# A decoder trunk's last feed-forward: down projection kept feature-major, the residual turned inside the last matmul groups

## Chip, cores and metric

The kernel runs on one core of a Trainium2 chip. The metric is the device time of one execution in microseconds. The kernel before has a median of 1202.2 us over three runs, from 1201.6 to 1202.57.

## The reference

Two layers over 512 tokens of width 1024, everything in float32. Layer 0 mixes tokens with forgetting attention, layer 1 with differential attention, and each adds cross-attention into 256 memory tokens. Every layer ends like this, and this is where the change lies:

```python
x = x + mix @ w_out[layer]
x = x + swiglu(rmsnorm(x, ffn_norm_g[layer]), w_gate_up[layer], w_down[layer])
...
return rmsnorm(x, final_norm_g)
```

Here `swiglu` is `(silu(h @ w_gate) * (h @ w_up)) @ w_down`, with 2816 hidden columns. The result of the last `rmsnorm` is stored with tokens as rows.

## The kernel before, in words

Activations lie feature-major: 128 features on the partitions, 512 tokens along the row, eight such blocks for width 1024. Each float32 operand is split into a high and a low part in the matmul type `fp32r`, and a product of two operands is three matmuls: high by high, low by high, high by low. The high part is a cast on ACT, the low part a subtraction on DVE, so every weight piece passes ACT, then DVE, before its low part can be used.

**Output projection** (`out_proj`, lines 588 to 614). Four quarters `o` of 256 output features, in PSUM tiles with the tags `acc`, `sc`, `y` and `tr`, one after the other. Each quarter is 48 matmuls of 512 columns (lines 199 to 201), over four weight chunks in the order 6, 0, 2, 4. For chunks 0 and 4 (`by_dma`), ACT writes the negated high part (L180), and a POOL DMA adds the raw weights onto it (L182); for the others, ACT casts (L165) and DVE subtracts (L166). After a quarter, DVE adds the residual (L603, L604), ACT multiplies by the norm's gain (L608), and `make` (L560 to L570) builds the operands of the feed-forward: `xh`, `xl`, and the sums `sh`, `sl`. Before the fourth quarter, `ahead()` loads the first three gate-and-up weight tiles (`FirstThree`); two of them get a second load added onto the first by POOL (L797).

**Residual.** In layer 0 it stays feature-major in `qs.block`, and its squares are summed on ACT and DVE (`squares`, L237 and L238). In layer 1 each block of the new residual is put into a scratch tile, turned to rows by four PE transposes (L619, into PSUM, 32 in all), copied to `res` by ACT (L620), and squared by row (L625); `norm_of_rows` brings the norm back to columns with a fp32 matmul (L637).

**Feed-forward** (`ffn`). Eleven quads of 256 hidden columns, gate and up together. Each quad is seven products of 24 matmuls of 256 columns (lines 835 to 837). The first three of the first quad (`first products` below: `acc`, `y` and `sc`, 72 matmuls) are put in program order after the output projection, and the tile scheduler lets some of them go ahead of it. Each quad's `p` copy (L881) follows its first product. Down projection pieces are filled in between the products of later quads (`fill`): in layer 0 feature-major, 12 matmuls of 512 columns (lines 943 to 945) per piece and an add on DVE; in layer 1 token-major, 24 matmuls of 256 columns (lines 934 to 936) and an add on DVE (L939). Pieces of the first group are half as long. In layer 1 the last four hidden blocks' share is computed by `final` (L975): for each of four token tiles and two halves, 12 matmuls of 512 columns (lines 991 to 993), DVE adds the residual row (L996), ACT squares (L998), DVE multiplies by the gain (L1005), then scales and stores.

**What sets the order.** The tile scheduler lays out each engine's queue, in order, from the program's order and its estimate of when things are ready; `with behind(pe)` keeps what stands in it behind the PE instruction issued last. Each engine then runs its queue strictly in order, and a waiting instruction holds all behind it.

## Time and profile before

| | before |
|---|---|
| median of three runs | 1202.2 us |
| profiled execution | 1206.7 us |
| its span | 1204.9 us |
| PE busy | 1168.8 us, 97% |
| DVE busy | 993.7 us, 82% |
| ACT busy | 662.8 us, 55% |
| POOL busy | 159.1 us, 13% |

PE is TensorE's matmuls, PEld its weight loads, DVE VectorE, ACT ScalarE, POOL GpSimd. The span runs from the first to the last instruction of the profiled execution; the execution's own time is 1.8 us longer. Times inside the trace count from the span's start. A matmul's length in the timeline overlaps the next one; the distance between starts is what it costs.

### The profile page before, as it was taken

Reading aid. Unit: us, or ns where it says so; the run is one execution under the profiler, and the core shown is the slowest. Engines: PE = TensorE matmul, PEld = TensorE weight load, DVE = VectorE, ACT = ScalarE, POOL = GpSimd, SP = SyncE. Lnnn points to the kernel's source line nnn. Section 1 sums busy time; section 2 is a strip of 40 time slices with the busy share of each in tenths; the row PEclk is TensorE's granted clock in tenths of the full one; section 3 lists DMA queues with packets and bytes.
Section 4 is the critical chain, followed back from the end, with each engine's and each line's share of the span. In section 5 each row is a group of like instructions: output and inputs, shape, how many; then the busy total and the mean of one; then the engine's idle time right before and its main releaser. Section 6 shows DMA issues by size and latency. Waiting matters only on the chain.

```text
span 1204.9 us, 21021 instructions
## 1 busy us (share of the span) xinstructions
PE 1168.8 (97%) x7854; PEld 1064.8 (88%) x7854; DVE 993.7 (82%) x1708; ACT 662.8 (55%) x1207; POOL 159.1 (13%) x154
## 2 busy tenths in 40 slices
PE   8999999999999999999999999997999999999997
PEld 7888888779999999999887888876899999999996
DVE  5879987789997787778789999977699878777776
ACT  7658776665443333333456979776554333333334
POOL 0002001121221111110001020112121111111000
PEclk9999999999999999999999999998999999999999
DMA  7533233466786666664133234455668666656512
GB/s 237 143 84 88 72 84 97 126 142 157 177 204 162 154 153 157 153 154 120 57 111 115 76 103 121 105 148 106 157 158 199 162 148 158 152 144 152 148 53 88
DMA packets 163065, 160.46 MB, mean 133 GB/s; under 512 B 12993, under 2 KB 152698, under 8 KB 162962
## 3 DMA queue, kind: packets, MB, share of 16 engines
q1 hardware_dynamic: 136722, 131.83, 36.7%
q0 software_dynamic: 26240, 27.27, 15.7%
q8 instruction: 62, 1.02, 0.4%
q14 instruction: 41, 0.34, 0.1%
HBM read 142.23 MB, written 2.10 MB: 120 GB/s over the span
## 4 chain that ended last, share of the span: by engine, by line
PE 74%; DVE 10%; ACT 5%; DMA 5%; issue 4%; SPq 1%; POOL 0%; ACTq 0%; DVEq 0%; POOLq 0%
PE acc L837 4%; PE acc L835 4%; PE acc L836 4%; PE y L837 4%; PE y L836 4%; PE y L835 4%; PE tr L943 3%; PE tr L944 3%; PE tr L945 3%; PE sc L836 3%; PE sc L837 3%; PE sc L835 3%; PE tr L936 3%; PE tr L934 3%; PE tr L935 3%
## 5 line engine op out<-in xcount | busy, mean ns | idle before, releaser
L228 ACT CAST fhi<-raw 128x1024 fp32r<-128x1024 f32 (+1 forms) x202 | 208.1, 1034 | 283.4 <-PE sc L837 100.9
L229 DVE TENSOR_TENSOR flo<-raw,fhi 128x1024 fp32r<-128x1024 f32 (+1 forms) x202 | 241.2, 1198 | 33.5 <-ACT fhi L228 33.4
L797 POOL DMA_DIRECT2D raw<-in_w_gate_up_dram x88 | 107.4, 1455 | 472.1 <-DMA raw<-in_w_gate_up_dram 288.5
L170 ACT ACTIVATE whi<-raw,gains 128x256 fp32r<-128x256 f32 (+1 forms) x192 | 86.6, 503 | 38.6 <-PE acc L201 22.0
L835 PE MATMUL acc<-xh,fhi 128*128 128x256 f32 x352 | 100.2, 285 | 5.6 <-ACT xh L228 5.6
L837 PE MATMUL acc<-xl,fhi 128*128 128x256 f32 x352 | 100.2, 285 | 0.6 <-DVE xl L229 0.5
L171 DVE SCALAR_TENSOR_TENSOR wlo<-raw,gains,whi 128x256 fp32r<-128x256 f32 (+1 forms) x192 | 87.2, 493 | 16.4 <-ACT whi L170 14.7
L836 PE MATMUL acc<-xh,flo 128*128 128x256 f32 x352 | 99.2, 282 | 0.0
L936 PE MATMUL tr<-flo,ah 128*128 128x256 f32 x288 | 81.3, 282 | 0.0
L934 PE MATMUL tr<-fhi,ah 128*128 128x256 f32 x288 | 81.1, 282 | 0.0
L935 PE MATMUL tr<-fhi,al 128*128 128x256 f32 x288 | 81.1, 282 | 0.0
L835 PE MATMUL y<-sh,fhi 128*128 128x256 f32 x256 | 72.7, 284 | 1.7 <-ACT sh L228 1.7
L835 PEld LDWEIGHTS acc<-xh,fhi 128*128 128x128 f32 x352 | 67.2, 191 | 7.0 <-ACT xh L228 6.5
L837 PE MATMUL y<-sl,fhi 128*128 128x256 f32 x256 | 72.8, 284 | 0.2 <-DVE sl L229 0.2
L836 PE MATMUL y<-sh,flo 128*128 128x256 f32 x256 | 72.6, 284 | 0.0
L943 PE MATMUL tr<-ah,fhi 128*128 128x512 f32 x176 | 69.2, 393 | 0.0
L944 PE MATMUL tr<-ah,flo 128*128 128x512 f32 x176 | 69.1, 393 | 0.0
L945 PE MATMUL tr<-al,fhi 128*128 128x512 f32 x176 | 68.8, 392 | 0.0
L837 PEld LDWEIGHTS acc<-xl,fhi 128*128 128x128 f32 x352 | 67.1, 191 | 1.6 <-DVE xl L229 1.4
L836 PEld LDWEIGHTS acc<-xh,flo 128*128 128x128 f32 x352 | 67.3, 191 | 0.4
L199 PE MATMUL acc<-xh,whi 128*128 128x512 f32 x168 | 66.7, 398 | 0.2 <-DVE qk L732 0.2
L200 PE MATMUL acc<-xh,wlo 128*128 128x512 f32 x168 | 66.3, 395 | 0.0
(482 smaller groups left out, 3787.6 us busy)
## 6 DMA issues: line engine op xcount, KB each, us to landing
raw<-in_w_gate_up_dram SPq DMA_DIRECT2D x220, 256.0 KB, 3.3
raw<-in_w_gate_up_dram POOLq DMA_DIRECT2D x88, 256.0 KB, 5.9
raw<-in_w_down_dram SPq DMA_DIRECT2D x80, 256.0 KB, 3.7
raw<-in_w_out_dram SPq DMA_DIRECT2D x32, 256.0 KB, 3.2
raw<-in_a_w_in_dram SPq DMA_DIRECT2D x48, 128.0 KB, 2.3
raw<-in_w_kv_shared_dram SPq DMA_DIRECT2D x24, 256.0 KB, 3.2
raw<-in_w_mem_kv_dram SPq DMA_DIRECT2D x16, 256.0 KB, 3.0
raw<-in_a_w_in_dram SPq DMA_DIRECT2D x16, 256.0 KB, 3.8
```

The costliest lines, as they stand in the source:

```text
L228: act.copy(h, src)
L229: dve.tensor_sub(l, src, f32(h))
L797: pool.dma_start(t[:, k : k + 2], plus[:, k : k + 2], accum_op=ALU.add)
L835: pe.matmul(o, hi[:, e, uc], ah, start=u == 0 and e == 0, stop=False)
L836: pe.matmul(o, lo[:, e, uc], ah, start=False, stop=False)
L837: pe.matmul(o, hi[:, e, uc], al, start=False, stop=u == 1 and e == NP - 1)
L934: pe.matmul(o, h[:, tc_], hi[:, k], start=t % 2 == 0 and k == 0, stop=False)
L935: pe.matmul(o, l_[:, tc_], hi[:, k], start=False, stop=False)
L936: pe.matmul(o, h[:, tc_], lo[:, k], start=False, stop=t % 2 == 1 and k == nk - 1)
L943: pe.matmul(b, hi[:, k, oc], h, start=k == 0, stop=False)
L944: pe.matmul(b, lo[:, k, oc], h, start=False, stop=False)
L945: pe.matmul(b, hi[:, k, oc], l_, start=False, stop=k == nk - 1)
```

## The change

In layer 1 the residual now stays feature-major, as in layer 0: squares are summed by `squares`, the norm is `finish_norm` for both layers, and `turn_rows`, `row_squares` and `norm_of_rows` are gone. The down projection is feature-major in both layers: 432 matmuls of 512 columns replace 864 of 256. In `final`, four plain fp32 matmuls of a residual block by the identity are added to each PSUM group, 32 in all, so that the residual is turned and added there; ACT squares and DVE multiplies straight from PSUM. And the first products of the first quad stand in a `with behind(pe)`, in both layers: they are queued behind the output projection's last matmul.

```diff
...
     def out_proj(l, yh, yl, order, qs, sc, ahead):
 
         acc = tmp("xacc")
-        late, xg = [], None
         for o in range(4):
             bs = two_banks(("acc", "sc", "y", "tr")[o])
             if o == 3:
                 ahead()
             project([(w_out[l], o * 256, 256)], None, yh, yl, bs, NKB, order=order, by_dma=(0, 4))
-            for f in late:
-                f()
-            late = []
+            xg = sc.full("g")
             for j in range(2):
                 kb = 2 * o + j
-                xn = qs.block(kb) if l == 0 else sc.next_half()
+                xn = qs.block(kb)
                 dve.tensor_add(xn, bs[j], f32(xh[:, kb]))
                 dve.tensor_add(xn, xn, f32(xl[:, kb]))
-                if j == 0:
-                    xg = sc.full("g")
                 g = gains[:, G_FFN[l] + kb : G_FFN[l] + kb + 1]
                 act.activation(xg[:, j], xn, AF.Copy, scale=g)
-                if l == 0:
-                    squares(xn, acc, kb == 0)
-                else:
-                    late.append(lambda kb=kb, xn=xn: turn_rows(kb, xn, qs.rows()))
+                squares(xn, acc, kb == 0)
             qs.make(o, xg, sc.full("u").rearrange("p a c -> p (a c)")[:, : 3 * H])
-        return acc, late
...
+        return acc
...
             bp1, bp7, bp6 = bank("acc"), bank("y"), bank("sc")
             if q == 0:
-                for es in (range(NP - 1), range(NP - 1, NP)):
-                    product(bp1, "a11", w.w11, es)
-                    product(bp7, "s3", w.wt3, es)
-                    product(bp6, "s2", w.wt2, es)
                 with behind(pe):
-                    if last:
-                        for f in late:
-                            f()
-                        row_squares(qs.rows(), ss, 1)
-                    else:
-                        finish_norm(acc, False, bank("tr"))
+                    for es in (range(NP - 1), range(NP - 1, NP)):
+                        product(bp1, "a11", w.w11, es)
+                        product(bp7, "s3", w.wt3, es)
+                        product(bp6, "s2", w.wt2, es)
+                with behind(pe):
+                    finish_norm(acc, False, bank("tr"))
             else:
...
                 b = bank("tr")
-                if last:
-                    for t in (2 * (i % 2), 2 * (i % 2) + 1):
-                        tc_, o = slice(t * P, (t + 1) * P), b[:, (t % 2) * H : (t % 2) * H + H]
-                        for k, (h, l_) in enumerate(a):
-                            pe.matmul(o, h[:, tc_], hi[:, k], start=t % 2 == 0 and k == 0, stop=False)
-                            pe.matmul(o, l_[:, tc_], hi[:, k], start=False, stop=False)
-                            pe.matmul(o, h[:, tc_], lo[:, k], start=False, stop=t % 2 == 1 and k == nk - 1)
-                    t0 = 2 * (i % 2)
-                    dst = qs.rows()[:, t0 : t0 + 2, c * 256 : c * 256 + 256]
-                    dve.tensor_add(dst, halves(b), dst)
-                    return
                 oc = slice((i % 2) * P, (i % 2) * P + P)
                 for k, (h, l_) in enumerate(a):
                     pe.matmul(b, hi[:, k, oc], h, start=k == 0, stop=False)
...
-        final(w, blocks_of(GROUPS[-1]), qs.rows(), ring, sc)
-
-    def final(w, a, xtok, ring, sc):
+        final(w, blocks_of(GROUPS[-1]), qs, ring, sc)
+
+    def final(w, a, qs, ring, sc):
...
                     pe.matmul(o, h[:, c], hi, start=k == 0, stop=False)
                     pe.matmul(o, l_[:, c], hi, start=False, stop=False)
-                    pe.matmul(o, h[:, c], lo, start=False, stop=k == len(a) - 1)
+                    pe.matmul(o, h[:, c], lo, start=False, stop=False)
+                for i in range(4):
+                    x = qs.block(4 * e + i)[:, t * P : (t + 1) * P]
+                    pe.matmul(o[:, i * P : (i + 1) * P], x, ident, start=False, stop=i == 3)
                 for i, c in enumerate(cols):
                     if c.start // 512 == e:
-                        dve.tensor_add(xo[:, c], o[:, c.start - e * 512 : c.stop - e * 512], xtok[:, t, c])
+                        oc = o[:, c.start - e * 512 : c.stop - e * 512]
                         q = work()[:, :n]
-                        act.activation(q, xo[:, c], AF.Square, accum_out=s2[:, i : i + 1])
+                        act.activation(q, oc, AF.Square, accum_out=s2[:, i : i + 1])
+                        dve.tensor_mul(xo[:, c], oc, fg[:, c])
...
             act.activation(ry, ry, AF.Exp, scale=-0.5)
-            for c in cols:
-                dve.tensor_mul(xo[:, c], xo[:, c], fg[:, c])
             dve.tensor_mul(ra, ry, ry)
...
```

The change's new lines are L796 to L798 for the quad products, L593, L594 and L596 for what were L603, L604 and L608, L562 to L565 for L565 to L568, L780 for L819, and L931 to L936 for the last share.

PE's queue at the fourth quarter of layer 1's output projection. `tr` is its output, `whi` and `wlo` the parts of its weights, `sc` a first product. Before:

```order
L835 MATMUL sc_9800<-sh_9319,fhi_9665 128x256 [waits Activation_49]
L836 MATMUL sc_9800<-sh_9319,flo_9666 128x256 [waits DVE_49]
L837 MATMUL sc_9800<-sl_9320,fhi_9665 128x256
L835 MATMUL sc_9800<-sh_9319,fhi_9665 128x256
L836 MATMUL sc_9800<-sh_9319,flo_9666 128x256
L837 MATMUL sc_9800<-sl_9320,fhi_9665 128x256
L200 MATMUL tr_9641<-yh_b,wlo_9672 128x512 [waits DVE_49]
L201 MATMUL tr_9641<-yl_b,whi_9671 128x512
L200 MATMUL tr_9642<-yh_b,wlo_9672 128x512
```

After, from the end of the third quarter:

```order
L201 MATMUL y_9528<-yl_b,whi_9586 128x512
L199 MATMUL tr_9627<-yh_b,whi_9657 128x512 [waits Activation_49]
L199 MATMUL tr_9628<-yh_b,whi_9657 128x512
L200 MATMUL tr_9627<-yh_b,wlo_9658 128x512 [waits DVE_49]
L201 MATMUL tr_9627<-yl_b,whi_9657 128x512
L200 MATMUL tr_9628<-yh_b,wlo_9658 128x512
```

Before, 30 first products stand between the quarter's two L199 and its first L200 with the low part. Now that L200 is the third instruction after the third quarter, and the first products follow the quarter's 48th matmul. In layer 0 the move is smaller: eight first products go from ahead of the last ten output matmuls to behind them.

DVE's queue in the same place, around the subtraction L166 that makes this low part. Before:

```order
L566 TENSOR_TENSOR g_9624<-g_9624 128x256 [waits DVE_49]
L229 TENSOR_TENSOR flo_9666<-raw_9643,fhi_9665 128x1024 [waits Activation_49]
L567 TENSOR_TENSOR u_9630<-g_9624 128x256 [waits DVE_49]
L229 TENSOR_TENSOR xl<-g_9624,xh 128x512 [waits Activation_49]
L568 TENSOR_TENSOR u_9630<-g_9624,u_9630 128x256 [waits DVE_49]
L166 TENSOR_TENSOR wlo_9672<-raw_9669,whi_9671 128x512 [waits DMAHW5_49,DMASW7_49]
L166 TENSOR_TENSOR wlo_9709<-raw_9706,whi_9708 128x512 [waits DMAHW7_49,DMASW6_49,DMASW0_49]
L229 TENSOR_TENSOR sl_9320<-u_9630,sh_9319 128x768 [waits Activation_49]
```

After:

```order
L563 TENSOR_TENSOR g_9603<-g_9603 128x256 [waits DVE_49]
L229 TENSOR_TENSOR flo_9647<-raw_9632,fhi_9646 128x1024 [waits DMASW3_49,DMASW2_49]
L564 TENSOR_TENSOR u_9616<-g_9603 128x256 [waits DVE_49]
L229 TENSOR_TENSOR xl<-g_9603,xh 128x512 [waits Activation_49]
L565 TENSOR_TENSOR u_9616<-g_9603,u_9616 128x256 [waits DVE_49]
L780 TENSOR_TENSOR raw_9629<-raw_9629,raw_9632 128x1024
L229 TENSOR_TENSOR sl_9320<-u_9616,sh_9319 128x768 [waits Activation_49]
L166 TENSOR_TENSOR wlo_9658<-raw_9655,whi_9657 128x512 [waits DMAHW5_49,DMASW7_49]
L229 TENSOR_TENSOR flo_9652<-raw_9629,fhi_9651 128x1024 [waits Activation_49]
L166 TENSOR_TENSOR wlo_9695<-raw_9692,whi_9694 128x512 [waits DMAHW7_49,DMASW6_49,DMASW0_49]
```

Before, L166 stands ahead of the third quarter's `sl`; now it stands behind it, and 24 instructions lie between the `sl` of the first quarter and it: two `sl` of 768 columns, eleven of 512, eight of 256 and three of 1024. That first-quarter `sl` waits for ACT's `sh`, which ACT has behind the same cast of a POOL-loaded tile (`fhi`, L228) as before.

PE's queue in `final`, at the end of the first token tile's first half. Before:

```order
L991 MATMUL tr_13609<-fhi_13591,ah_13578 128x512
L992 MATMUL tr_13609<-fhi_13591,al_13579 128x512
L993 MATMUL tr_13609<-flo_13592,ah_13578 128x512
L991 MATMUL acc_13610<-fhi_13597,ah_13215 128x512 [waits Activation_49]
L992 MATMUL acc_13610<-fhi_13597,al_13216 128x512
```

After:

```order
L931 MATMUL tr_13116<-fhi_13098,ah_13085 128x512
L932 MATMUL tr_13116<-fhi_13098,al_13086 128x512
L933 MATMUL tr_13116<-flo_13099,ah_13085 128x512
L936 MATMUL tr_13116<-ident,res_9321 128x128 x4
L931 MATMUL acc_13117<-fhi_13104,ah_12770 128x512 [waits Activation_49]
```

Four matmuls of `res` by `ident` now end each group.

## Rows read from the trace of the kernel before

**Rows 1.** The page, busy us (share of the span) and instructions of each engine.
```profile
PE 1168.8 (97%) x7854; PEld 1064.8 (88%) x7854; DVE 993.7 (82%) x1708; ACT 662.8 (55%) x1207; POOL 159.1 (13%) x154
```

**Rows 2.** Busy time by stretch: from:to, length, then the engines', clock, DMA.
```profile
core 0: us, PE busy (x) PEld busy (x) DVE busy (x) ACT busy (x) POOL busy (x), PEclk, DMA share, GB/s
828.60:838.80 10.20, 7.54 (x27) 6.13 (x28) 10.14 (x19) 8.76 (x19) 0.89 (x1) 0.50 0.16 51
...
850.20:958.90 108.70, 105.96 (x884) 104.90 (x883) 97.76 (x118) 53.79 (x68) 21.72 (x18) 1.00 0.74 180
958.90:1147.30 188.40, 188.40 (x1586) 188.40 (x1585) 148.90 (x157) 71.71 (x73) 26.55 (x22) 1.00 0.61 149
273.40:379.00 105.60, 105.00 (x789) 99.99 (x788) 98.57 (x116) 50.18 (x56) 21.66 (x18) 1.00 0.74 179
379.00:564.60 185.60, 185.60 (x1299) 173.49 (x1298) 148.79 (x157) 71.80 (x73) 26.56 (x22) 1.00 0.62 152
```

**Rows 3.** Timeline of PE, layer 1: start, length, line, [idle before <-releaser].
```profile
822.40 0.40 PE L201 MATMUL y<-yl_b,whi 128*128 128x512 f32 x1
...
828.57 0.58 PE L835 MATMUL acc<-xh,fhi 128*128 128x256 f32 x1 [4.54 <-ACT xh L228]
...
832.75 0.58 PE L835 MATMUL y<-sh,fhi 128*128 128x256 f32 x1 [1.68 <-ACT sh L228]
...
839.19 0.50 PE L200 MATMUL tr<-yh_b,wlo 128*128 128x512 f32 x1
```

**Rows 4.** Chain of waits (start, us, what), then ACT's timeline, layer 1.
```profile
815.29 8.07 DMA raw<-in_w_gate_up_dram
...
823.44 1.05 ACT L228 CAST fhi<-raw 128x1024 fp32r<-128x1024 f32 x1 [4.50 <-DMA raw<-in_w_gate_up_dram]
...
825.43 0.83 ACT L228 CAST sh<-u 128x768 fp32r<-128x768 f32 x1
```

**Rows 5.** Timeline of DVE, layer 1, operands of the output projection's quarters.
```profile
825.64 1.22 DVE L229 TENSOR_TENSOR flo<-raw,fhi 128x1024 fp32r<-128x1024 f32 x1
826.78 0.95 DVE L229 TENSOR_TENSOR sl<-u,sh 128x768 fp32r<-128x768 f32 x1
827.65 0.68 DVE L603 TENSOR_TENSOR u<-y,xh 128x512 f32<-128x512 f32 x1
828.25 0.41 DVE L565 TENSOR_TENSOR u<-g 128x256 f32<-128x256 f32 x1
828.58 0.68 DVE L229 TENSOR_TENSOR xl<-g,xh 128x512 fp32r<-128x512 f32 x1
...
838.45 1.29 DVE L166 TENSOR_TENSOR wlo<-raw,whi 128x512 fp32r<-128x512 f32 x2
```

**Rows 6.** Timelines of PE and of ACT, layer 0, last quarter.
```profile
263.62 0.50 PE L200 MATMUL tr<-yh_a,wlo 128*128 128x512 f32 x1 [1.51 <-DMA wlo<-raw]
...
269.51 0.28 PE L835 MATMUL acc<-xh,fhi 128*128 128x256 f32 x1
...
270.81 0.51 PE L200 MATMUL tr<-yh_a,wlo 128*128 128x512 f32 x1 [0.21 <-DMA wlo<-raw]
...
265.72 0.63 ACT L180 ACTIVATE wlo<-raw 128x512 fp32r<-128x512 f32 x1
```

**Rows 7.** Timeline of PE, layer 1; last row: line L637's weight loads (ns, min/median/max).
```profile
814.99 1.07 PE L619 MATMUL tr<-ident,u 128*128 128x128 f32 x8
815.81 0.48 PE L201 MATMUL y<-yl_b,whi 128*128 128x512 f32 x1
...
874.15 1.16 PE L637 MATMUL tr<-work,ones 128*128 128x128 f32 x8 [2.07 <-DVE work L636]
875.07 0.36 PE L837 MATMUL acc<-xl,fhi 128*128 128x256 f32 x1
...
L637 PEld LDWEIGHTS tr<-work,ones x8: 187/192/193, 874.2 to 874.9; 128*128 128x128 f32 x8
```

**Rows 8.** Timeline of DVE and ACT at the end of the kernel.
```profile
1198.06 0.75 DVE L996 TENSOR_TENSOR u<-sc,res 128x256 f32<-128x256 f32 x2 [0.47 <-PE sc L993]
...
1198.52 0.42 ACT L998 ACTIVATE work<-u 128x256 f32<-128x256 f32 x1 [1.39 <-DVE u L996]
```

More of the change, by code (lines that the diff above doesn't have):

```diff
@@ L547, in block @@
             return self.x[:, kb * S : (kb + 1) * S]
-        def rows(self):
-            return self.x.rearrange("p (t d) -> p t d", t=NT)
         def operand(self, form, e):
@@ L575, in __init__ @@
         def __init__(self, pl):
-            self.pl, self.n = pl, 0
+            self.pl = pl
         def half(self, tag):
@@ L582, in full @@
             return self.pl.tile([P, 2, S], F32, tag=tag, name=nm(tag))
-        def next_half(self):
-            self.n += 1
-            return self.half(("p1", "u2", "u3")[self.n % 3])
     def out_proj(l, yh, yl, order, qs, sc, ahead):
         acc = tmp("xacc")
-        late, xg = [], None
         for o in range(4):
@@ L820, in __init__, with ffn @@
             self.wt2 = ring.parts(self.b11)
-    def ffn(l, acc, last, qs, late, ring, sc, pl, ahead):
+    def ffn(l, acc, last, qs, ring, sc, pl, ahead):
         raw, parts = ring.load, ring.parts
@@ L842, in ffn @@
         gated = {}
-        if last:
-            ss = tmp("ss", (P, 2, NT))
-            row_squares(qs.rows(), ss, 0)
         def quad(q, down):
@@ L888, in quad @@
             fill(1)
-            if q == 0 and last:
-                with behind(pe):
-                    norm_of_rows(ss)
             dve.tensor_add(b11, b11, b21)
@@ L1024, in output_and_ffn @@
             ahead = []
-            acc, late = out_proj(
+            acc = out_proj(
                 l, yh, yl, [6, 0, 2, 4], qs, sc, lambda: ahead.append(FirstThree(l, 0, ring))
@@ L1030, in output_and_ffn @@
             ring.far = open_pool(fs, f"f{l}", "right")
-            acc = ffn(l, acc, last, qs, late, ring, sc, open_pool(fs, f"a{l}"), ahead)
+            acc = ffn(l, acc, last, qs, ring, sc, open_pool(fs, f"a{l}"), ahead)
         if not last:
```

21 lines of the change are left out of this document (removed).

## Prediction

> **What bounds the kernel now.** I read the page's busy times first: PE (TensorE) works in 97% of the span, DVE in 82% [rows 1]. So a change counts where it adds or removes PE instructions, or makes PE wait. The busy time by stretch says where each is [rows 2]. Two stretches are fully packed in both layers: from the fifth quad's `p` copy to the eleventh's, PE is busy for 188.4 of 188.40 us in layer 1 and 185.6 of 185.60 us in layer 0. There only the number and kind of matmuls matter. The one place in layer 1 with a large hole is the passage from output projection to feed-forward: from 828.6 to 838.8 PE works 7.54 of 10.20 us, and at a granted clock of 0.50, which is the 1.2 GHz level; before and after it stands at 1.00.
>
> The timeline of PE shows why [rows 3]: the third quarter's last product starts at 822.40; then PE idles 4.54 us before 828.57 and 1.68 us before 832.75, and the fourth quarter's first low-part product (L200 with `wlo`) comes only at 839.19. The chain of waits names the start of it: a POOL accumulating load of `raw` takes 8.07 us from 815.29, ACT sits 4.50 us until its cast at 823.44, and the cast of `sh` is at 825.43 [rows 4]. DVE stands behind that cast, then works through third-quarter operands up to the two L166 subtractions at 838.45, the first of which makes that low part [rows 5]. So DVE's queue ends last there; its start-to-start times are 1.14 us for 1024 columns, 0.87 for 768, 0.60 for 512 and 0.33 for 256.
>
> **The change, part by part.**
>
> (a) End of the output projection, layer 1. Before, 30 first products ran while PE waited for the low part (they lie ahead of it in PE's order). Now nothing but two L199 products can. Worse, L166 has moved back in DVE's order: 24 instructions lie between the `sl` that waits for ACT's `sh` and L166: two more `sl`, eleven of 512 columns (among them square sums of layer 1, new on DVE), eight of 256, three of 1024. From 825.7 (the cast at 825.43 is now ahead by one `xh`, its end stays near) the sum with that first `sl` is 3×0.87 + 11×0.61 + 8×0.34 + 3×1.14 = 15.5 us; ACT's own queue (two gains, a square, a cast between each pair) adds about 0.8 us where the third quarter's gained block is awaited, and L166 itself takes 0.69. The low part is then there at 842.7, not 839.2: +3.5. PE will have been idle some 20 us, so I expect 1.2 GHz again when it resumes. The clock rose at 838.8, after 3.7 us of unbroken work from 835.1 [rows 2, 3]; the same after 842.7 costs 1.9 us of full-speed work. Bounds: nothing (the clock stays) and 5.1 us (the 10.2 us that the low level lasted in all). The next chunk's low part is accumulated by POOL; ACT issues its half at about 842.2, and in layer 0 PE got such a part 5.1 us after ACT's L180 started (265.72 to 270.81) [rows 6]: 847.3, when PE, at half speed, has done the ten products ahead of it by 846.9. +0.4. Together **+5.8** (3.5 to 9).
>
> (b) From there to the fifth quad's copy. The stretches of [rows 2] that begin at 850.2 and 273.4 begin where the last output product ends. Layer 1 now does what layer 0 does: 105.60 us there, 108.70 before, so −3.1. In this go 16 of the 32 transposes (L619, eight in 0.82 us), and the late wait of 2.07 us for DVE's L636 [rows 7]; the down matmuls become half as many of twice the width. But layer 0 had done eight first products (from 269.51 on, about 0.12 each [rows 6]) before its last ten output products; layer 1 now has done none: +0.95. Bounds −3.1 and −1.5; I take **−2.2**.
>
> (c) Fifth to eleventh quad: the same instructions as in layer 0: 185.6 − 188.4 = **−2.8**. Both are packed, so nothing hides this. By the loops this stretch holds 24 down pieces of 24 matmuls, and three more follow it: 3/24 of 2.8, **−0.35**.
>
> (d) The last share: 32 more matmuls, `x` block by identity, in plain fp32, on a PE that ends the kernel. The nearest row is L637, plain fp32, 128×128: four such matmuls (eight records) start at 874.15, and the next product at 875.07, 0.23 us each [rows 7]. 32 × 0.23 = **+7.4**. The lower bound is the price of a transposition of the same block, 0.10 us, 3.3 in all. For the upper bound, L637 loads the same `ones` for all its matmuls, and here each has its own block of `x` to load, in two loads; if those of 0.19 us [rows 7] were not covered by matmuls, a turn would take 0.38, 12.3 in all. I take L637, as it is the same kind of instruction and shape, and it too has two loads each. DVE's adds L996 fall away; they lay beside PE.
>
> The Trainium skill, Perfetto Trace Analysis, section Transposes, says that a logical transposition should use the transpose rather than a standard matmul. By this the change pays PE more than the 32 transposes it takes out (some 3.3 us); the two rows, 0.10 and 0.23, agree.
>
> (e) The tail. When PE's last product is done, DVE adds at 1198.06 and ACT squares at 1198.52 [rows 8]. Now ACT squares from PSUM when DVE would have begun: **−0.45**. The multiplication by the gain moves to DVE beside it.
>
> (f) Layer 0. Its eight first products filled the wait for the accumulated low part (270.81, idle 0.21 even so [rows 6]); now that wait is bare. At most 0.95; later waits in its first quads may take some back: **+0.6** (0 to 0.95).
>
> SP's and POOL's queues keep their order but for two down-weight loads, moved by one place: nothing, as these stretches are packed by PE.
>
> Sum: 5.8 − 2.2 − 2.8 − 0.35 + 7.4 − 0.45 + 0.6 = **+8.0 us**. The profiled execution took 1206.7, so 1214.7; the median of the runs, 1202.2, lies 4.5 below it, and the sum carried there gives **1210.2 us**.
>
> **The rivals.**
>
> *Faster: the low part is not late.* In layer 0 the same order ran the last quarter with a wait of 1.51 us before 263.62 and the one at 270.81, with the clock at 1.00. If layer 1 did that, the 48 products (0.23 each) would start by 822.6 and end near 835.4, where before they ended at 850.2: −14.8 in place of +5.8, and the total −12.6, **1189.6**. It decides at L166 ready by about 834.7, 8 us sooner than my chain. For it: the same code in layer 0. Against it: the load that holds ACT until 823.44 [rows 4] hangs on POOL's queue, whose order is unchanged, and DVE's 15.5 us come after it. 5%.
>
> *No change: the turn is cheap.* If a matmul by identity costs no more than a transposition, (d) is 3.3; with the clock term at nothing the sum is +2.0, **1204**. For it: L619 has the same operands. Against it: L637. 10%, 6% of it within 0.2%.
>
> *Dear: the weight loads of the turns are bare.* Then (d) is 12.3, the total +12.9, and the time **1215**. For it: new weights for each of the 32. Against it: L637 pays 0.23 with as many loads, and the matmuls ahead in the queue leave time to load. 7%. The Trainium skill, TensorE: Matmul & The Clock Gate, section Terms, gives transposition as 4× faster for fp32; by that figure and the 0.10 of L619, an estimate, a turn would take 0.41 and all 13.1, while the rows 0.23 and 0.10 are a ratio of 2.3.
>
> *The clock stays low longer.* At 10.2 us of half speed, 3.2 more: **1213.4**. It comes after a longer idle time than the one before. 15%.
>
> **How the numbers follow.** My forecast with its own bounds has 63%. 0.2% of the time, 2.4 us, is about what a measurement can tell from no change. Faster by more than that: the first rival and a little of small gains that I don't see, 0.06. Within: the cheap turn, or a low part that comes as before with all later gains, 0.09. Slower: the rest, 0.85. The range leaves out the faster rival and the dearest end: 1203.5 to 1216.
>
> **What would show it.** In the changed profile the first L200 of the fourth quarter in layer 1 should start at 842 to 843, not 839.19 [rows 3], the windows should show half clock after it for 3 to 5 us, the fifth to eleventh quad should take 185.6 us, the identity matmuls 0.23 us each, and the square of the last tile should start right after the last matmul. A low part before 838, or identity matmuls near 0.10 or 0.4, would make me wrong; so would packed stretches that don't come down to layer 0's.

## The result and the profile after

The changed kernel takes **1216.39 us** (median of four, 1215.8 to 1217.06), the kernel before 1202.38 beside it: a ratio of **1.0117**, with a 95% interval of 1.01 to 1.0135. That is 14.0 us slower; forecast were 8.0 us and 1210.2, with 1216.0 as the upper end. The sign and the mechanism named for it hold, the size does not.

The profiled execution of the changed kernel took 1215.8 us, so it is 9.1 us above the one that the prediction read (1206.7), near the 8.0. Most of the miss is thus not seen when these two traces are laid side by side, and the runs below search for it.

The page of the changed kernel, busy time, the line that answers to [rows 1]:

```profile
PE 1169.7 (96%) x7448; PEld 1048.2 (86%) x7448; DVE 994.1 (82%) x1700; ACT 659.4 (54%) x1190; POOL 159.1 (13%) x154
```

PE has 406 instructions fewer and works 0.9 us more. Busy time by stretch of the changed kernel, in the columns of [rows 2]: three pieces of layer 1's passage, then the stretches that answer to the last four rows there:

```profile
core 0: us, PE busy (x) PEld busy (x) DVE busy (x) ACT busy (x) POOL busy (x), PEclk, DMA share, GB/s
826.20:840.60 14.40, 0.00 (x0) 0.00 (x0) 14.40 (x25) 9.28 (x16) 0.00 (x0) 0.50 0.02 2
840.60:846.50 5.90, 5.87 (x14) 4.62 (x15) 1.71 (x2) 0.64 (x2) 1.77 (x2) 0.50 0.76 173
...
854.10:962.00 107.90, 106.94 (x797) 101.94 (x796) 99.04 (x116) 50.15 (x56) 21.72 (x18) 1.00 0.74 180
962.00:1148.90 186.90, 186.90 (x1298) 174.72 (x1298) 148.86 (x157) 71.86 (x73) 26.58 (x22) 1.00 0.62 150
269.60:377.80 108.20, 107.21 (x797) 102.00 (x796) 99.11 (x116) 50.33 (x57) 21.72 (x18) 1.00 0.73 175
377.80:564.60 186.80, 186.80 (x1298) 174.62 (x1297) 148.76 (x157) 71.80 (x72) 26.59 (x22) 1.00 0.62 150
```

In the passage PE does nothing for 14.4 us while DVE is busy in all of them, and then runs 5.9 us at the low clock. The last row is the one that nobody had named: layer 0's packed stretch, whose instructions the change leaves alone, went from 185.6 [rows 2] to 186.8, with the same count of matmuls to one.

The passage in the timelines of PE, ACT and DVE of the changed kernel (they answer to [rows 3 to 5]):

```profile
821.90 0.39 PE L201 MATMUL y<-yl_b,whi 128*128 128x512 f32 x1
823.79 0.74 PE L199 MATMUL tr<-yh_b,whi 128*128 128x512 f32 x2 [1.50 <-ACT whi L165]
840.63 0.79 PE L200 MATMUL tr<-yh_b,wlo 128*128 128x512 f32 x1 [16.10 <-DVE wlo L166]
```

```profile
822.17 1.05 ACT L228 CAST fhi<-raw 128x1024 fp32r<-128x1024 f32 x1 [2.71 <-DMA raw<-in_w_gate_up_dram]
823.12 0.61 ACT L165 CAST whi<-raw 128x512 fp32r<-128x512 f32 x1
823.64 0.83 ACT L228 CAST sh<-u 128x768 fp32r<-128x768 f32 x1
```

```profile
824.51 0.96 DVE L229 TENSOR_TENSOR sl<-u,sh 128x768 fp32r<-128x768 f32 x1 [2.59 <-ACT sh L228]
...
839.89 0.69 DVE L166 TENSOR_TENSOR wlo<-raw,whi 128x512 fp32r<-128x512 f32 x1
```

DVE waits for ACT's `sh` and then needs 15.4 us (824.51 to 839.89) to reach L166: the prediction had 15.5 for this and 0.8 more for waits, which did not come.

### The profile page after: what moved, and what is told of

Its sections match the earlier page's. It is cut to its first block, busy times and chain, and to the rows that moved or that the text cites. A ratio compares the mean times of both kernels' runs of the same rounds, so it can differ in the third digit from the quotient of the medians.

```text
span 1213.9 us, 20180 instructions
## 1 busy us (share of the span) xinstructions
PE 1169.7 (96%) x7448; PEld 1048.2 (86%) x7448; DVE 994.1 (82%) x1700; ACT 659.4 (54%) x1190; POOL 159.1 (13%) x154
## 4 chain that ended last, share of the span: by engine, by line
PE 76%; DVE 11%; DMA 6%; ACT 4%; issue 3%; SPq 1%; POOL 0%; ACTq 0%; DVEq 0%; POOLq 0%
PE tr L884 6%; PE tr L885 6%; PE tr L883 6%; PE acc L797 4%; PE acc L798 4%; PE acc L796 4%; PE y L796 4%; PE y L797 4%; PE y L798 4%; PE sc L797 3%; PE sc L798 3%; PE sc L796 3%; PE acc L201 3%; PE acc L200 3%; PE acc L199 3%
## 5 line engine op out<-in xcount | busy, mean ns | idle before, releaser
L228 ACT CAST fhi<-raw 128x1024 fp32r<-128x1024 f32 (+1 forms) x202 | 207.8, 1034 | 283.4 <-PE sc L798 100.6
L884 PE MATMUL tr<-ah,flo 128*128 128x512 f32 x320 | 125.9, 393 | 0.0
L885 PE MATMUL tr<-al,fhi 128*128 128x512 f32 x320 | 125.5, 393 | 0.0
L883 PE MATMUL tr<-ah,fhi 128*128 128x512 f32 x320 | 125.3, 392 | 0.0
L798 PE MATMUL acc<-xl,fhi 128*128 128x256 f32 x352 | 99.3, 282 | 0.0
L796 PE MATMUL acc<-xh,fhi 128*128 128x256 f32 x352 | 99.1, 282 | 0.0
L796 PE MATMUL y<-sh,fhi 128*128 128x256 f32 x256 | 72.3, 283 | 0.0
L798 PE MATMUL y<-sl,fhi 128*128 128x256 f32 x256 | 72.1, 282 | 0.0
L885 PEld LDWEIGHTS tr<-al,fhi 128*128 128x128 f32 x320 | 60.1, 188 | 13.1
L883 PEld LDWEIGHTS tr<-ah,fhi 128*128 128x128 f32 x320 | 60.3, 188 | 10.5
L884 PEld LDWEIGHTS tr<-ah,flo 128*128 128x128 f32 x320 | 60.2, 188 | 10.4
L796 PEld LDWEIGHTS acc<-xh,fhi 128*128 128x128 f32 x352 | 66.5, 189 | 0.9
L199 PE MATMUL acc<-xh,whi 128*128 128x512 f32 x168 | 66.6, 397 | 0.2 <-DVE qk L693 0.2
L798 PEld LDWEIGHTS acc<-xl,fhi 128*128 128x128 f32 x352 | 66.6, 189 | 0.1
L200 PE MATMUL acc<-xh,wlo 128*128 128x512 f32 x168 | 66.3, 394 | 0.0
```

Source lines behind the costliest of these rows:

```text
L199: pe.matmul(o, hi[:, k, c], ah[:, kb, :n], start=first, stop=False)
L200: pe.matmul(o, lo[:, k, c], ah[:, kb, :n], start=False, stop=False)
L228: act.copy(h, src)
L796: pe.matmul(o, hi[:, e, uc], ah, start=u == 0 and e == 0, stop=False)
L798: pe.matmul(o, hi[:, e, uc], al, start=False, stop=u == 1 and e == NP - 1)
L883: pe.matmul(b, hi[:, k, oc], h, start=k == 0, stop=False)
```

## Experiments

Each run was timed beside the kernel before, whose medians there were 1203.7 to 1204.3, with single executions between 1199.8 and 1208.8; ratios are to those. Beside the change the median had been 1202.4, so differences to the change are given twice where it matters: of the medians as they are, and by the ratios, times 1203 us. The two differ by 1 to 2 us, and a single difference is known no better than that. `a_ring64` and the runs with 32, 128 and 192 bytes have one execution each, beside one of 1203.25.

**Is the profiled execution of before a usual one?** `before_again` is the kernel before, unchanged.

> The kernel before, unchanged, to see another profiled execution: the one shown took 1206.7 us, 4.3 above the median of 1202.4, while the executions of the changed kernel lie close to their median. Theory 1: the 4.3 us lie in the passage between output projection and feed-forward of layer 1, which hangs on one transfer (8.07 us from issue to landing there); a usual execution spans about 1200.5, with the first low-part product of the fourth quarter at 835 or earlier in place of 839.2, and the packed stretches unchanged (188.4 and 185.6). Rival 2: the excess is spread over the packed matmul stretches; then the passage ends at 839 again and the fifth to eleventh quad of layer 1 takes 184 to 186. Rival 3: the profiled execution is always that much longer; then this one spans about 1205 again.

It spans 1201.9 us, 3.0 less than the execution first read. All three explanations fall. Rival 3 had it at 1205 again; theory 1 falls because the passage has the same length (from the output projection's first product to its last 72.65 us there, 72.80 here), and rival 2 because the packed stretches have it too:

```profile
376.20:561.70 185.50, 185.50 (x1298) 173.35 (x1298) 148.72 (x157) 71.80 (x72) 26.56 (x22) 1.00 0.63 151
955.80:1144.20 188.40, 188.40 (x1586) 188.40 (x1585) 148.92 (x157) 71.81 (x72) 26.56 (x22) 1.00 0.62 149
```

Of the 3.0 us, 2.8 are there by the end of layer 0's output projection: its last product starts at 273.01 in the first execution and at 270.18 here, and the projection itself took 63.27 us there, 61.15 here. In the first execution the granted clock was 0.50 from 214.2 to 217.6 us, inside that projection; here it was 1.00 all through it. So the trace that the prediction read had about 3 us of early time that this one does not have, and against this one the difference of spans is 12.0 (1201.86 to 1213.90). Starts of the same instructions in the timelines, `before_again` against the changed kernel, divide it:

| stretch | forecast | before, again | changed | difference |
|---|---|---|---|---|
| layer 0: last output product to fifth quad's copy | +0.6 | 106.05 | 108.37 | +2.3 |
| layer 0: fifth to eleventh quad's copy | 0 | 185.51 | 186.83 | +1.3 |
| layer 1: output projection, first to last product | +5.8 | 72.80 | 76.41 | +3.6 |
| to the fifth quad's copy | −2.2 | 107.95 | 108.15 | +0.2 |
| fifth to eleventh | −2.8 | 188.42 | 186.82 | −1.6 |
| to the last matmul's start | +7.05 | 50.34 | 57.44 | +7.1 |
| to the end | −0.45 | 7.30 | 7.60 | +0.3 |

These add to 13.2; the rest of the span before and between them gives back 1.2.

**What the queueing costs.** `a_no_queue` takes it out of the change, `b_queue` puts it into the kernel before:

```diff
-                with behind(pe):
-                    for es in (range(NP - 1), range(NP - 1, NP)):
-                        product(bp1, "a11", w.w11, es)
...
+                for es in (range(NP - 1), range(NP - 1, NP)):
+                    product(bp1, "a11", w.w11, es)
```

> The change without the queueing of the first products (the scheduler places them again, 30 of them ahead of the low part in layer 1, eight ahead of the last ten output products in layer 0). DVE's order stays that of the change, so the low part comes as late as there. Theory 1 (PE idle in the passage and the longer half clock are the price of the queueing): 30 x 0.12 = 3.6 us of products are done in the idle time, the clock rises earlier, 1 to 2 us more: 1210 to 1212, against 1216.4. Rival (the low part's lateness alone decides, and what is done earlier is lost to waits in the first quads): within 1 us of the change, 1215.5 to 1216.5.

> The kernel before with only the queueing of the first products added (both layers): the residual is turned by transposes and the down projection token-major as before. PE can do none of the 30 first products in layer 1's passage; DVE's order is that of before, so the low part comes no later. Theory 1: 3.6 us of products move behind the output projection, and the clock is low for 1 to 2 us of work more: plus 4 to 6, 1206 to 1208. Rival (later waits in the first quads shrink by as much, since their operands have more time): within 1 us of 1202.4.

`a_no_queue`: 1213.85 us, ratio 1.0084 (1.0064 to 1.0104), 2.5 below the change, or 4.0 by the ratios: less than theory 1 said, more than the rival. In the two traces the passage is no shorter for it (76.70 against 76.41 us); from the last output product to the fifth quad's copy 1.5 us are gained in layer 0 and 1.3 in layer 1. `b_queue`: 1209.0, ratio 1.0048 (1.0027 to 1.0069), 5.3 above the kernel before, as theory 1 said. Its PE:

```profile
828.85 1.27 PE L199 MATMUL tr<-yh_b,whi 128*128 128x512 f32 x2 [5.61 <-ACT res L620]
...
838.99 0.79 PE L200 MATMUL tr<-yh_b,wlo 128*128 128x512 f32 x1 [8.87 <-DVE wlo L166]
```

The low part comes no later than before (838.99 against 839.19 in [rows 3]); what is lost is the work that used to fill the wait. In `a_no_queue` the first products cannot fill it so well, since their own operands come late from the same DVE (one waits 7.32 us for `flo`, and the low part comes only at 841.76).

**What the turn costs.** `a_no_turn` leaves the turns out, so the second residual is missing from its output:

```diff
...
-                for i in range(4):
-                    x = qs.block(4 * e + i)[:, t * P : (t + 1) * P]
-                    pe.matmul(o[:, i * P : (i + 1) * P], x, ident, start=False, stop=i == 3)
...
```

> The change with the 32 fp32 matmuls by the identity left out of the last share, so that the second residual is missing from the output: the price of the turn alone. Theory 1 (0.23 us each, as in line L637): 7.3 us less than the change, about 1209. Rival (bare weight loads, 0.38 each): 12.3 less, 1204. Rival (as cheap as a transposition, 0.10): 3.3 less, 1213.

1210.7 us, ratio 1.0051 (1.0035 to 1.0066): 5.7 below the change, or 7.9 by the ratios, on either side of the 7.3 expected. The trace is sharper. From the eleventh quad's copy to the last matmul it takes 50.26 us, with the turns 57.44: 7.18 for 32, **0.224 us each**. In the timeline of the changed kernel four turns (eight records) stand like this, and the product behind them loses another 0.09 to the next start (0.31 where 0.23 is usual):

```profile
1184.46 1.06 PE L936 MATMUL acc<-ident,res 128*128 128x128 f32 x8
1185.28 0.48 PE L932 MATMUL y<-fhi,al 128*128 128x512 f32 x1
1185.59 0.39 PE L933 MATMUL y<-flo,ah 128*128 128x512 f32 x1
```

**The slower packed stretches.** In the change `ss` and `nrm`, two small scratch tiles that took 64 bytes of each partition, are gone. The built programs place the tiles behind them 64 bytes lower, among them three of the four slots that weight halves rotate through (first bytes in a partition); the fourth slot, `xh` and `xl` lie where they did:

```
        before   changed  a_ring64
xh       18144     18144     18144
sh       70336     70272     70272
fhi     137920    137856    137920
```

`a_pad64` puts 64 unused bytes in their place, `b_shift` takes 64 away from the kernel before; all queues keep their order.

```diff
+    tmp("pad", (P, 16))
     wp = open_pool(streams, "wa", "right")
```

```diff
-            ss = tmp("ss", (P, 2, NT))
+            ss = [tmp("fs0", (P, NT), bufs=2) for _ in range(2)]
...
-        r = tmp("nrm", (P, NT))
+        r = tmp("fs1", (P, NT), bufs=2)
```

> The change with one unused scratch tile of 64 bytes per partition put back in the place of the two small ones that went (ss and nrm), so that every later tile, the weight halves fhi and flo among them, has the address of before; the queues of all engines hold the same instructions in the same order. Theory 4 (the 256-column products run at a pace that depends on where fhi and flo lie in SBUF; in the traces layer 0's fifth to eleventh quad, whose instructions the change leaves alone, went from 185.52 to 186.83 us, and with the queueing alone added to the kernel before it stayed at 185.51): that stretch takes 185.5 again in layer 0 and 185.5 in layer 1 in place of 186.82, and with some 3700 such products in all the time falls by 4 to 5 us, to about 1212. Rival (the slower pace comes with the new work of the change itself, not with addresses): no difference, 1216.4, and 186.8 in both stretches.

> The kernel before with its two small tiles ss and nrm placed in others that exist already, which moves all later tiles down by 64 bytes to the addresses of the change; same instructions, same order. Theory 4 (addresses): layer 0's stretch from the fifth to the eleventh quad takes 186.8 us, layer 1's 189 to 191, and the time rises by 4 to 5 us, to about 1208. Rival (the pace belongs to the change's work): 185.5, 188.4 and 1203.5, as before.

`a_pad64`: **1212.75 us**, ratio 1.0072 (1.0048 to 1.0097), 3.6 below the change, or 5.4 by the ratios. `b_shift`: **1208.0 us**, ratio 1.0036 (1.0022 to 1.0051), 3.9 above the kernel before. The same two stretches as above, of layer 0 and of layer 1, first in `a_pad64`, then in `b_shift`:

```profile
380.10:565.60 185.50, 185.50 (x1298) 173.35 (x1298) 148.75 (x157) 71.74 (x72) 26.59 (x22) 1.00 0.61 152
962.30:1147.80 185.50, 185.50 (x1298) 173.35 (x1297) 148.72 (x157) 71.72 (x73) 26.56 (x22) 1.00 0.61 151
```

```profile
378.70:565.50 186.80, 186.80 (x1298) 174.61 (x1297) 148.76 (x157) 71.72 (x72) 26.59 (x22) 1.00 0.62 150
960.00:1149.60 189.60, 189.60 (x1586) 189.60 (x1586) 149.29 (x157) 71.65 (x72) 26.55 (x22) 1.00 0.60 148
```

With the addresses of before the change has 185.5 in both layers; with those of the change the kernel before has 186.8 and 189.6. Theory 4 holds both ways, and its rival falls. By kind of product, in layer 0's stretch, the mean distance between starts says which ones: `xh` by `flo` 117.4 ns before and 120.4 in the change, `xl` by `fhi` 117.8 and 120.1, `xh` by `fhi` 117.9 and 119.3, the products of `sh` and `sl` within 0.2 of each other. When each product is matched with the slot of its weights in the built program, `xh` by `flo` went from 116.4 to 120.7 ns with weights in the three slots that moved, and from 119.3 to 119.6 with weights in the fourth, which did not.

Four more runs, of one execution each, ask for the pattern:

```diff
-            ring = Ring(open_pool(fs, f"n{l}"))
+            near = open_pool(fs, f"n{l}")
+            near.tile([P, 16], F32, tag="pad", name=nm("pad"))
+            ring = Ring(near)
```

is `a_ring64`; the other three are `a_pad64` with 32, 128 and 192 bytes.

> The change with 32 bytes of unused scratch, half of what the two small tiles took; same instructions, same order. If the pace of the 256-column products hangs on the addresses of the later tiles, layer 0's stretch from the fifth to the eleventh quad lies off both 185.5 (64 bytes) and 186.8 (0 bytes), or equals one of them if only coarser bits of the address count. If two tiles more or fewer made the difference by something else: 186.8.

> The change with 128 bytes of unused scratch. If the pace repeats with the address at 128 bytes, the stretch takes 186.8 as with none; if any later place is as good as that of before, 185.5; a third value means a finer or longer pattern.

> The change with 192 bytes of unused scratch. If the pace repeats at 128 bytes, the stretch takes 185.5 as with 64.

> The change with the 64 bytes put at the head of the weight ring alone, so that raw, fhi, flo and behind them ah, al lie as in the kernel before, and sh, sl, res and the smaller tiles as in the change. If what counts is where fhi and flo lie relative to xh and xl (which never move), the products of xh and xl run at the pace of before and those of sh and sl at another; the stretch comes to 185 to 186. If it is where sh, sl or res lie: 186.8.

Layer 0's stretch takes 185.40, 185.80 and 186.33 us with 32, 128 and 192 bytes (times 1211.94, 1214.06 and 1215.48): no simple repeat. `a_ring64` is below all, and below the 185 to 186 expected (time 1207.27):

```profile
376.90:561.10 184.20, 184.20 (x1298) 172.28 (x1297) 148.78 (x157) 71.80 (x72) 26.56 (x22) 1.00 0.63 153
956.60:1140.90 184.30, 184.30 (x1298) 172.38 (x1298) 148.88 (x157) 71.81 (x73) 26.58 (x22) 1.00 0.63 153
```

There the `xh` and `xl` products run at 117.4 to 117.7 ns as before, and those of `sh` and `sl` at 116.7 to 117.1 where they had 118.8 to 119.4. Since `xh` never moves, and `sh` lies as in the change, it is the place of the weight halves against the operands that counts here: with the fourth slot's weights, which no run moves, the products of `sh` and `sl` run at 118.5 to 118.7 ns in `a_ring64` (117.8 to 118.0 in the change), and with the three others at 116.1 to 116.6 (119.3 to 119.8 in the change). `a_ring64` also moves the raw weights and `ah` and `al`, which lie in or behind the same ring. The rule behind the pace stays open.

**The tail.** `a_tail`:

```diff
-                        dve.tensor_mul(xo[:, c], oc, fg[:, c])
+                        if t < NT - 1:
+                            dve.tensor_mul(xo[:, c], oc, fg[:, c])
...
             act.activation(ry, ry, AF.Exp, scale=-0.5)
+            if t == NT - 1:
+                for c in cols:
+                    e = c.start // 512
+                    dve.tensor_mul(xo[:, c], bs[2 * t + e][:, c.start - e * 512 : c.stop - e * 512], fg[:, c])
```

> The change with the last token tile's four multiplications by the gain put behind its squares. In the trace of the change ACT and DVE take turns on the last PSUM tile (square 1206.61, multiplication 1207.12, square 1207.58, multiplication 1208.09), and from the last turn to the end it takes 0.45 us longer than from the last matmul to the end before. Theory: the squares follow one another and the multiplications lie beside the chain; 0.7 to 0.9 us less than the change, about 1215.6. Rival (the turns are not the bound of the tail): no difference within 0.3.

The end of the changed kernel, then that of `a_tail`:

```profile
1206.61 0.39 ACT L941 ACTIVATE work<-sc 128x256 f32<-128x256 f32 x1 [2.25 <-PE sc L936]
...
1207.12 0.42 DVE L942 TENSOR_TENSOR u<-sc,fgain 128x256 f32<-128x256 f32 x1 [2.31 <-ACT work L941]
1207.58 0.38 ACT L941 ACTIVATE work<-sc 128x256 f32<-128x256 f32 x1 [0.49 <-DVE u L942]
...
1208.09 0.42 DVE L942 TENSOR_TENSOR u<-sc,fgain 128x256 f32<-128x256 f32 x1 [0.54 <-ACT work L941]
```

```profile
1207.73 0.39 ACT L941 ACTIVATE work<-sc 128x256 f32<-128x256 f32 x1 [2.86 <-PE sc L936]
...
1208.10 0.38 ACT L941 ACTIVATE work<-sc 128x256 f32<-128x256 f32 x1
...
1208.60 0.16 DVE L945 TENSOR_REDUCE fs<-fs 128x1 f32<-128x4 f32 x1 [2.94 <-ACT work L941]
```

In the change ACT and DVE wait for one another, as the built program has it, though both only read the PSUM tile; in `a_tail` the squares follow one another, and the stretch from the last matmul to the end falls from 7.60 to 6.80 us, as the theory said. The whole time, 1216.9 with ratio 1.0111 (1.0089 to 1.0133), does not show it: 0.5 above the change, 0.7 below it by the ratios (in the profiled execution the passage was 1.6 us longer, 77.99 against 76.41). For the time the run is inconclusive.

**All three together.** `a_all` is the change with the 64 bytes, without the queueing, with the tail's new order.

> The change with the 64 bytes put back, the first products not queued, and the tail as in the run before this one: what is left is the down projection, the second residual's turn by fp32 matmuls, and the later low part. If the three terms add up (4 to 5, 2.5 and 0.8): 1208 to 1209, still 4 to 6 above the kernel before, because the turns cost 7.3 and the down projection gives back 2.9 and the transposes 3. If the terms share a cause (the queueing's price falls with the pace): 1210 to 1212.

1208.49 us, ratio 1.0036 (1.0021 to 1.0052): 7.9 below the change, where the single runs give 3.6 and 2.5 and the tail's stretch 0.8, in all 6.9. By the ratios it is 9.7, against 5.4, 4.0 and 0.7, in all 10.1. So the terms add, as closely as these times can tell.

**The passage itself.** ACT waits for one transfer with `sh` queued behind, DVE's `sl` waits for `sh`, and L166 stands behind `sl`. `a_late` (and `b_late` for the kernel before, `c_late` for `a_all`) moves the split of that tile behind the output projection, for ACT and DVE at once:

```diff
...
-            self.w11 = ring.parts(self.b11)
+            self.w11, self.ring = ring.parts(self.b11), ring
+            if not late:
+                self.rest()
+
+        def rest(self):
-            self.wt3 = ring.parts(self.t3)
+            self.wt3 = self.ring.parts(self.t3)
             dve.tensor_add(self.b11, self.b11, self.t3)
-            self.wt2 = ring.parts(self.b11)
+            self.wt2 = self.ring.parts(self.b11)
...
+            if q == 0:
+                w.rest()
...
```

> The change with one piece of program order moved, in both layers: the split of the second first-weight tile (the one that POOL adds a second load onto), its sum with the first and the split of that sum stand behind the output projection, not ahead of its fourth quarter; the loads stay where they are. ACT's cast that waits for that transfer then stands behind the first quarter's sh, and DVE's first low-part subtraction ten places earlier. Theory 1 (ACT and DVE, held by that transfer, make the low part late; the length of the passage follows from it): the low part comes at 831 to 833 in place of 840.6, PE idles 9 to 10 us in place of 18; 7 to 9 us less than the change, 1207.5 to 1209.5. Rival (DVE's queue alone is the bound, the transfer is hidden behind it): 1 us less at most.

> The same move in the kernel before, nothing else. There DVE has no square sums in layer 1, and its first low-part subtraction moves 21 places up. Theory 1: the low part, at 839.2 before, comes at 828 to 831; 8 to 11 us less, 1192 to 1196. Rival (what PE gains there is lost again to waits in the first quads, whose operands DVE then makes later): 1198 to 1203.

> The change with all four mends: the 64 bytes put back, the first products not queued, the tail in the other order (as in the run with all three), and the moved split. Theory 1: that run's 1208.5 less 7 to 9: 1200 to 1201. Rival (the first products that fill the passage now stand in front of the low part): 1204 to 1206.

`a_late`: 1204.36 us, ratio 0.9998 (0.9985 to 1.0011), 12.0 less than the change (14.3 by the ratios) and more than theory 1 gave. `b_late`: **1195.92**, 0.9922 (0.9904 to 0.994), 8.1 less than the kernel before, at the end of theory 1's range. `c_late`: 1198.11, 0.9952 (0.9935 to 0.9968), 2 below what theory 1 gave. The low part in `a_late`, PE's timeline, then ACT's `sh` and the wait that is late next, then DVE:

```profile
833.61 0.79 PE L200 MATMUL tr<-yh_b,wlo 128*128 128x512 f32 x1 [10.63 <-DVE wlo L166]
```

```profile
821.11 0.83 ACT L228 CAST sh<-u 128x768 fp32r<-128x768 f32 x1
...
826.27 0.62 ACT L181 CAST whi<-raw 128x512 fp32r<-128x512 f32 x1 [2.07 <-DMA raw<-in_w_out_dram]
```

```profile
822.64 0.94 DVE L229 TENSOR_TENSOR sl<-u,sh 128x768 fp32r<-128x768 f32 x1
...
832.88 0.68 DVE L166 TENSOR_TENSOR wlo<-raw,whi 128x512 fp32r<-128x512 f32 x1
```

From the output projection's first product to its last it takes 67.97 us, 8.4 less than in the change. Another 2 us are in layer 0, where the same move was made: its fifth quad's copy is at 375.88, in the change at 377.78.

The low part comes at 833.61, after 10.6 us of idle time (831 to 833 and 9 to 10 were expected). That is 11.5 us after the third quarter's last product, in the change 18.7. Of these 7.2 us, `sl` gives 2.1 by starting earlier, and the way from `sl` to L166 gives 5.1: 10.2 us in place of 15.4, with 13 instructions between in place of 24. So the lateness is DVE's queue more than ACT's wait, and `b_late` shows it plainly:

```profile
815.58 0.68 DVE L166 TENSOR_TENSOR wlo<-raw,whi 128x512 fp32r<-128x512 f32 x1
...
821.62 0.96 DVE L229 TENSOR_TENSOR sl<-u,sh 128x768 fp32r<-128x768 f32 x1 [4.56 <-ACT sh L228]
```

Here ACT waits for another transfer (5.07 us) and `sh` comes later than before, 4.1 us after the third quarter's last product in place of 2.9 to 3.0. But L166 now stands ahead of `sl`, and the output projection takes 64.89 us in place of 72.80.

**A cheaper turn.** `c_turn_r` splits the second residual and turns it by 64 fp32r products in place of 32 fp32 ones:

```diff
...
-                    x = qs.block(4 * e + i)[:, t * P : (t + 1) * P]
-                    pe.matmul(o[:, i * P : (i + 1) * P], x, ident, start=False, stop=i == 3)
+                    for part in (xh, xl):
+                        x = part[:, 4 * e + i, t * P : (t + 1) * P]
+                        pe.matmul(o[:, i * P : (i + 1) * P], x, identr, start=False, stop=i == 3 and part is xl)
...
```

> As the run before this one, and the second residual split into a high and a low fp32r part (eight casts on ACT, eight subtractions on DVE, after the last quad) and turned by 64 fp32r matmuls by the identity in place of 32 plain fp32 ones. Theory (a 128-column fp32r product costs half of a 256-column one, 0.06 us, so 64 cost 3.8 against 7.2): 3.4 us less than the run before this one. Rival (a short product is bound by its weight load, 0.11 to 0.12 us): no gain. A third: ACT and DVE are late with the parts, and PE waits in the last share.

1198.51 us, ratio 0.9949 (0.9931 to 0.9967): nothing gained over `c_late`. PE does not wait for late parts either: from the eleventh quad's copy to the last matmul it takes 57.25 us, in `c_late` 57.13. The second rival holds; the first ones of a group in the timeline:

```profile
1187.73 0.22 PE L947 MATMUL sc<-u,xh 128*128 128x128 f32 x1
1187.79 0.27 PE L947 MATMUL sc<-u,xl 128*128 128x128 f32 x1
1187.90 0.28 PE L947 MATMUL sc<-u,xh 128*128 128x128 f32 x1
1188.01 0.28 PE L947 MATMUL sc<-u,xl 128*128 128x128 f32 x1
```

The first is followed after 0.06 us; its weight load starts at 1187.50, beside the long product ahead of it. The others start 0.11 us apart, nearly as far as 256 columns do (0.117 to 0.120), so two cost what one plain fp32 turn costs.

**The best of both.** `c_ring` is `c_late` with the addresses of `a_ring64`, `b_ring` is `b_late` with them.

> The change with first products not queued, the tail in the other order and the moved split, and with the addresses of the run a_ring64 (fhi, flo, ah, al 64 bytes further from sh, sl, and as far from xh, xl as before). There the stretch of layer 0 took 184.24 us, 1.3 less than with the addresses of before; if that holds here, both stretches take 184.2 and the time is 4 to 5 us below the 1198.1 of the run c_late: 1193 to 1194.5. If the pace is tied to the change's order of work: 1198.

> The kernel before with the moved split and the addresses of a_ring64. Layer 0's stretch should take 184.2 as there; layer 1's, whose down projection is token-major with fhi and flo on the moving side, 186 to 188 where before it took 188.42; in all 3 to 5 us below the 1195.9 of the run b_late, 1191 to 1193. If the pace of the token-major products falls with this shift: 1195 to 1197.

`c_ring`: 1193.95 us, ratio 0.9916 (0.9902 to 0.9931). `b_ring`: **1189.21 us, ratio 0.9873** (0.9856 to 0.9889), 15 us below the kernel before and 2 below what was expected. Layer 0's and layer 1's stretch in `c_ring`, then in `b_ring`:

```profile
373.30:557.60 184.30, 184.30 (x1298) 172.35 (x1298) 148.80 (x157) 71.83 (x73) 26.56 (x22) 1.00 0.63 152
943.70:1127.90 184.20, 184.20 (x1298) 172.25 (x1297) 148.70 (x157) 71.77 (x72) 26.55 (x22) 1.00 0.63 153
```

```profile
373.70:557.90 184.20, 184.20 (x1298) 172.26 (x1297) 148.72 (x157) 71.79 (x72) 26.56 (x22) 1.00 0.63 153
945.60:1132.00 186.40, 186.40 (x1587) 186.40 (x1586) 148.92 (x157) 71.80 (x73) 26.56 (x22) 1.00 0.62 151
```

The pace goes with the addresses under either order of work. With all mends the feature-major version stays 4.7 us behind by the medians, 2.6 in the two traces: there it gains 2.1 in layer 1's stretch and 2.3 between output projection and fifth quad, and pays 7.2 for the turns.

## Why the prediction was right or wrong

**The step that failed** is in (c): "the same instructions as in layer 0: 185.6", and with it the silence on every other stretch. Layer 1's stretch did come down to layer 0's, but both took 186.8: same instructions in the same order do not mean the same pace when tiles go away ahead of them. Put back by 64 bytes, the change has 185.52 in both, the −2.9 that (c) meant. Between the two traces the five stretches with such products lose 4.5 us in all by these 64 bytes; the medians give 3.6 and the ratios 5.4. With the addresses of before the change costs a ratio of 1.0072, or 8.7 us; the forecast was 8.0. So this is the larger part of the miss of 6.0; the other terms, some too high and some too low, leave the rest.

**The carrying to the median** did no harm: it comes to 1202.2 and 8.0. But the trace that the terms were read from was 3.0 us longer than another one, 2.8 of it before 273 us, ahead of nearly all that the change touches. That hid part of the miss when the first two traces were compared; the medians are free of it.

**(a) The passage** was right in mechanism, and a little high. From the `sl` of [rows 5] to L166 DVE takes 15.4 us in each of the eight executions with the change's order and 11.7 in each of the three with the order of before, so the longer queue costs 3.7, where 3.5 were forecast for the low part. (The sum of 15.5 takes 0.61 and 0.34 us where the rows gave 0.60 and 0.33; that is 0.2 of it.) But `sl` began earlier in the change (the cast at 822.17 and not 823.44), so the low part came at 840.63, not 842.7. The half clock lasted 6 us after PE resumed, not 3.7 and not the 3 to 5 named as a sign, as the longer-clock rival had it in part. Between the output projection's first and last product the change's order took 75.3 to 78.0 us in eight executions, the order of before 71.9 to 72.8 in three; the means differ by 4.3, where 5.8 were forecast. Half of that lies ahead of the low part (2.2), half behind it (2.1). The rival that "the low part is not late" fell, though what it named is real: with the split moved, the passage loses 8.4 us.

**(b)** was +0.2 in place of −2.2. In `a_pad64` it is −0.7 (107.27 against 107.95), so 0.9 of the miss is the pace; another 1.2 is that the first execution took 109.12 us there, with the wait of 2.07 us in [rows 7] that I counted on getting back, and `before_again` 107.95, with a wait of 0.70 us in that place.

**(d) The turn** was right: 7.2 measured, 7.4 forecast, and both rivals on its price fell. The Trainium skill's rule in Perfetto Trace Analysis, section Transposes, to use the transpose for a logical transposition, agrees: 0.224 us against 0.10 in [rows 7]. The Trainium skill's factor of 4 for fp32 in TensorE: Matmul & The Clock Gate, section Terms, does not: it is 2.2 here.

**(e) The tail** had the wrong sign, +0.3 for −0.45. "The multiplication by the gain moves to DVE beside it" was the step: it does not lie beside the squares but takes turns with them. `a_tail` shows the forecast's −0.5 (6.80 against 7.30).

**(f) Layer 0** was +2.3 over that stretch, with the output projection ahead of it as long as in `before_again` (60.99 against 61.15 us). With the addresses of before, the queueing alone costs 1.35 there (`b_queue`, 107.40) and the change 1.6 (`a_pad64`, 107.67); the last 0.7 is pace. So (f) was too low by about 1, and the step was that "later waits in its first quads may take some back": the eight products cost their 0.95, and a later wait for `flo` grew, from 0.43 us before 297.38 in `before_again` to 0.96 before 298.21 in the change.

## What to carry to other kernels

Removing or adding even a small scratch tile moves the tiles behind it, and packed matmul streams may change pace by about a per cent (184.2 to 186.8 us here); compare a stretch whose instructions the change leaves alone before explaining one that it touches, and put padding back to keep the two apart. Work that filled a wait of PE was nearly free here, and queued behind the wait it cost its price. Before ordering products around a late operand, ask what makes it late, on every engine that it passes: here a short subtraction stood in DVE's queue behind operands of later products, and moving one tile's split out of its way gave 8 to 12 us.

## What was not expected of the hardware

A shift of 64 bytes in SBUF between weights and moving operand changed the start-to-start time of 256-column fp32r products by 1.4 to 3 ns of 118, alike in every execution profiled with the same addresses (185.5 against 186.8 us for 1298 matmuls); where both moved together, it did not. A shift of the weight ring against `sh` and `sl` gave 184.2. A 128-column fp32r product behind another one started 0.11 us after it, hardly sooner than a 256-column one. And executions of the same kernel before differed by up to 11 us (1199.8 to 1210.8), of which the two profiled ones show 2.8 arising before 273 us.
